# Query, key and attention weights turned by VectorE blocks and a DRAM round trip instead of TensorE, in a hybrid attention layer on one core

## The chip, the core and the metric

The kernel runs on one core of a Trainium2 chip. Five engines matter: TensorE (PE in the profile, with its weight loads as PEld), VectorE (DVE), ScalarE (ACT), GpSimd (POOL, which here only issues DMAs that add to their target) and SyncE (SP, which issues most DMAs). The metric is the device time of one execution in microseconds. A median over three runs is given.

## What is computed

One layer for 512 tokens of width 2048, in float32. The input is normalized and multiplied by one wide matrix. Its columns give, for three branches with four heads of 128 columns each, a query, a key, a value and a gate (4 x 128 columns a head), and for each branch 2048 merge gates.

```
A: p = softmax(q k^T / sqrt(128) + forget bias, causal);  o = p v     (q, k normalized)
B: p = softmax(q k^T / sqrt(128) + bias by distance);     o = p v     (q, k normalized)
C: p = stick-breaking weights of q k^T / sqrt(128);       o = p v
y      = o * silu(gate)                  for every head
merged = sum over branches of sigmoid(merge gate) * (y_branch @ w_up)
out    = x + merged @ w_out
```

The forget bias of A is a running sum over the log of a per-token gate that is computed from the input as well (the "forget sums").

## The kernel before, in words

**Matmuls.** Every float32 operand is split into an upper and a lower part of reduced precision, and a product is three matmuls (upper by upper, lower by upper, upper by lower), so a tile of 128x128 by 512 costs three. All large ones are issued by `mm` (line 266). The work is cut into *units*: each takes a weight chunk of 256x512 (512 KB), splits it on ACT into the upper part (`wh`, line 376) and on DVE into the lower part (`wl`, line 386), and multiplies. Two units are prepared ahead of the one that runs (`LA`, three buffers of `wh`, two of `wl`), and eight raw chunks (`raw`, `NR`) are loaded ahead on SP's queue (line 278).

**Input projection.** The 24 column groups of 512 (12 heads, 12 gate groups) are taken in this order: the first head plain (`first_head`, 9 units), the first gate group plain (8 units), and then eleven pairs of one gate group and one head (`head`). A pair is done by Strassen's scheme with seven products of four units each (`Strassen`, 28 units). The products come in the order 5, 1, 6, 7, 4, 2, 3 (`PLAIN`, line 592). Their sums are made in `after` (line 644): product 5 is copied from PSUM by ACT and kept for product 7; 7 and 4 finish the head's halves, 2 and 3 the gate group's. For four of the products the weight chunks are sums: those of 5 and 7 are summed by a second, adding DMA on POOL's queue (line 282), those of 6 and 3 by DVE (line 588). Finished gate groups are scaled and stored to DRAM (`spill`, line 1161), to be read again for the merge.

**Attention.** A head arrives as four tiles `c` of 128 tokens x (query, key, value, gate). For A and B, query and key are normalized (`norms`). `qk` turns query and key so that the head dimension lies on the partitions: four PE transposes into a PSUM bank each (`turned`, line 873), then ACT and DVE make the upper and lower part from PSUM. `values` splits the values block by block (lines 907 and 909). `gate` turns the gate in another way: DVE turns 32x32 blocks (line 920), SP stores them to DRAM (line 923), and four DMAs on ACT's queue (line 930) read them back so that the blocks land in their turned places; each piece read is one row of 32 numbers. The last head turns its gate on PE. `soft_scores` or `stick_scores` make the weights `p`, one block of 128 queries at a time, against 128 to 512 keys. `soft_trans` turns them on PE (line 1019; 4 + 3 + 2 + 1 turns a head) and splits them, and `av` multiplies with the values (lines 1107 to 1109). The last head adds its causal mask by a small matmul on PE (line 988), the other A heads on DVE (line 991).

**Order of the work.** The order of the instructions on PE, ACT and DVE is written out when the kernel is built, by a planner (`Flow`). Each piece of work is a generator that yields the engine and the time that it is taken to need, buffers, or events; the planner always takes the piece that can start first, by its own clock, and each engine then runs its queue in that order. A DMA has a planned landing time (`landing`, line 271):

```
        line[0] = max(line[0], ready) + 0.5
        line[1] = max(line[1], line[0] + 1.0) + kb / 370.0
        return line[1] + 1.5
```

If data land later than planned, the engine that has the reading instruction next in its queue stands, and everything behind it. SP and ACT issue DMAs in order too. Attention is hung onto the units by `at`: `stages` (line 1124) gives each step a distance in units from the point where the head is finished, by the offsets `OFF` (line 1523) for scores, turned weights and values.

**PSUM** has eight banks: four for products (`acc`), four for side work (`att`).

**After the projection** come 24 units for the up-projection with the merge gates, whose merged result is turned on PE too (line 1357, 64 turns), and two Strassen tasks of 28 units for the output.

Of the kernel before, what the change touches and what calls it, by code (L numbers as in the profile page):

```python
# [36 lines left out]
Q, K, V, G = 0, 1, 2, 3  # L37
# [126 lines left out]
def hybrid_kernel(  # L164
# [22 lines left out]
    pa = ctx.enter_context(tc.tile_pool(name="pa", bufs=4, space=PS))  # L187
    pt = ctx.enter_context(tc.tile_pool(name="pt", bufs=4, space=PS))
# [9 lines left out]
    t2s, atts, raws, xps = Slots(NT, KEPT), Slots(4), Slots(NR), Slots(NX)  # L198
    accs, wls = Slots(4), Slots(LA)
# [16 lines left out]
    def blk(i):  # L216
        return slice(i * P, (i + 1) * P)
# [62 lines left out]

    def add_up(to, src, ready, kb):
# [26 lines left out]
    onef, zerof, nu_f = tmpc[:, blk(0)], tmpc[:, blk(1)], tmpc[:, blk(2)]  # L308
# [5 lines left out]
    identb = cp.tile([P, P], BF16, name="identb")  # L314
    nc.vector.tensor_copy(identb, identf)

    mska = cp.tile([P, P], BF16, name="mska")
    nc.gpsimd.affine_select(out=nu_f, in_=zerof, pattern=[[-1, P]], base=0, channel_multiplier=1,
                            compare_op=ALU.is_ge, fill=NEG)
    nc.vector.tensor_copy(mska, nu_f)  # L320

# [270 lines left out]
    PLAIN = [(p, c) for p in (5, 1, 6, 7, 4, 2, 3) for c in range(CH)]  # L592

    class Strassen:
# [9 lines left out]
        def __init__(self, src, ops, done, order=PLAIN, other=(), rest=None):  # L604
            self.src, self.ops, self.done, self.rest = src, ops, done, rest
            self.order, self.other = order, other
            self.ps, self.ev = {}, {}
# [36 lines left out]
        def after(self, p, tb, slots):  # L644
# [8 lines left out]
            if p in (1, 5):  # L653
                yield t2s, 1
                c = t2("v" if p == 5 else "u")
                yield ACT, act_us(S)
                nc.scalar.activation(c, ps, AF.Copy)
                (v if p == 5 else u)[tb] = c
                give(slots)
                set_(self.event(p, tb))  # L660
# [9 lines left out]
            elif p == 7:  # L670
                yield self.event(6, tb)
                yield t2s, 1
                u3[tb] = t2("w")
                yield d
                add(u3[tb], u2[tb], ps)
                give(slots)
                yield self.event(5, tb)
                yield d
                add(u2[tb], u2[tb], v[tb])
                spawn(self.left("c12", tb, lambda r: add(u2[tb], u2[tb], r)), 4.0, flow.fin)  # L680
                yield d
                minus(v[tb], u3[tb], v[tb])
                spawn(self.left("c21", tb, lambda r: sub(u3[tb], r, u3[tb])), 4.0, flow.fin)
                spawn(self.left("c22", tb, lambda r: add(v[tb], v[tb], r)), 4.0, flow.fin)
                yield self.event("c22", tb)
                finished("c22", v[tb])
# [130 lines left out]
    class Head:  # L817
        def __init__(self, n, h, last=False):
            self.n, self.h, self.last = n, h, last
# [3 lines left out]
            self.c, self.t, self.ev, self.count = [None] * QB, {}, {}, {}  # L823

# [19 lines left out]
        def taken(self):  # L844

            if self.nth("taken", 4):
                give(t2s, QB)

# [19 lines left out]
        def turned(self, r):  # L868

            yield PE, 0.11 * QB  # L870
            ps = att()
            for tb in range(QB):
                nc.tensor.transpose(ps[:, blk(tb)], self.c[tb][:, blk(r)], identf)  # L873
            self.taken()
            return ps

        def qk(self, r):
            if self.n == C:
                yield from self.all_there()
            else:  # L880
                yield self.event("n", r)
            yield t2s, 2
            self.t[r] = pair_of("qk")
            yield atts, 1
            ps = yield from self.turned(r)
            h, lo = self.t[r]
            if self.n == C:
                yield from split(h, lo, ps, S)
            else:
# [3 lines left out]
                nc.scalar.activation(h, ps, AF.Copy, scale=g)  # L893
                yield DVE, dve_us(S)
                nc.vector.scalar_tensor_tensor(lo, ps, g, f(h), op0=ALU.mult, op1=ALU.subtract)
            give(atts)
            set_(self.event("p", r))

        def values(self):
            yield from self.all_there()  # L900
# [3 lines left out]
            for tb in range(QB):  # L904
                c = self.c[tb][:, blk(V)]
                yield ACT, act_us(P)
                nc.scalar.activation(h[:, blk(tb)], c, AF.Copy)
                yield DVE, dve_us(P)
                nc.vector.tensor_sub(lo[:, blk(tb)], c, f(h[:, blk(tb)]))
            self.taken()  # L910
            set_(self.event("v"))

        def gate(self):
            yield from self.all_there()
            yield t2s, 1
            if not self.last:
                t = t2("gt")
                for tb in range(QB):
                    yield DVE, 0.3
                    nc.vector.transpose(t[:, blk(tb)], self.c[tb][:, blk(G)])  # L920
                self.taken()
                gd = dp.tile([4 * QB, 32, P], F32, name=nm("gd"))
                nc.sync.dma_start(gd.rearrange("(t a) r c -> (a r) t c", a=4), t.rearrange("p (t c) -> p t c", t=QB))
                stored(t2s, 1, 256)
# [649 lines left out]
```

## Time and profile before

| what | value |
|---|---|
| runs | 1301.43 us median of 3 (1301.05 to 1301.47) |
| profiled execution: span of its instructions | 1300.1 us |
| instructions | 17368 |
| PE busy | 1294.1 us |
| DVE busy | 1069.5 us |
| ACT busy | 748.2 us |
| DMA moved | 284.39 MB, mean 219 GB/s |

The profile gives the profiled execution by its span; the median of the runs is 1.3 us above it. The profile's page counts each engine's busy time; issuing DMAs is not counted. A row of a group reads: line, engine, operation, output<-input, shapes, count | busy us, mean ns of one | idle time before it and who ended it. A row of the chain reads: start us, length us, what. A row of waits reads: who waited for whom: us in total, times, longest. A row of a window reads: from:to, its length, then busy us (and instructions) of PE, PEld, DVE, ACT and POOL, then PE's granted clock, the DMA engines' mean share and GB/s. A row of the DMA queues reads: packets, MB, share of the span of sixteen engines; a row of DMA issues ends with the KB of one and its median time from issue to landing.

### The profile page before, as it was taken

To read this page: it belongs to the slowest core of one execution; us is meant where nothing else is said; L and a number is where in the kernel's file an instruction comes from. 1 tells how busy PE (TensorE), PEld (TensorE's weight loads), DVE (VectorE), ACT (ScalarE), POOL (GpSimd) and SP (SyncE) were. 2 spreads that over 40 slices of the span, in tenths; PEclk is the share of its full clock that TensorE was granted. 3 is DMA by queue.
4 is the path that set the end of the run, shared out by engine and by line. 5 is a ranking of instruction groups with operands and counts; after the bars stand their busy time and mean duration, and the time that the engine had idled before them with its cause. 6 is when DMAs were issued, how large, how long until landed. Compare 5 with 4: busy or idle time off the path is not lost.

```text
span 1300.1 us, 17368 instructions
## 1 busy us (share of the span) xinstructions
PE 1294.1 (100%) x5941; PEld 1075.1 (83%) x5941; DVE 1069.5 (82%) x1607; ACT 748.2 (58%) x1259; POOL 92.0 (7%) x116
## 2 busy tenths in 40 slices
PE   9999999999999999999999999999999999999998
PEld 8888888888888888888888888888888888888887
DVE  7966797898989888898886886978879668698767
ACT  7745465565557646576466664666658546463442
POOL 0001000110011001110011000110000000000110
PEclk9999999999999999999999999999999999999999
DMA  9855687896788989888787777877796756738983
GB/s 358 256 147 145 185 230 194 230 239 215 218 238 237 250 236 272 236 240 240 205 249 175 222 213 191 252 162 208 224 282 194 264 194 196 177 93 258 250 245 126
DMA packets 124072, 284.39 MB, mean 219 GB/s; under 512 B 34368, under 2 KB 40144, under 8 KB 123984
## 3 DMA queue, kind: packets, MB, share of 16 engines
q1 hardware_dynamic: 83328, 221.42, 50.7%
q0 software_dynamic: 14976, 54.53, 23.1%
q10 hardware_dynamic: 25680, 7.34, 2.3%
q8 instruction: 46, 0.75, 0.2%
q14 instruction: 42, 0.34, 0.1%
HBM read 260.66 MB, written 22.59 MB: 218 GB/s over the span
## 4 chain that ended last, share of the span: by engine, by line
PE 99%; DMA 1%; DVE 0%; issue 0%; ACT 0%; ACTq 0%
PE acc L266 93%; PE att L1019 1%; PE att L873 1%; DMA gl<-u 1%; PE att L1109 1%; PE att L1108 1%; PE att L261 1%; PE att L262 1%; PE att L263 1%; PE att L1357 1%; PE att L1107 1%; PE att L430 0%; DVE s L702 0%; DVE u L1161 0%; DVE gt L920 0%
## 5 line engine op out<-in xcount | busy, mean ns | idle before, releaser
L376 ACT ACTIVATE wh<-raw 128x1024 fp32r<-128x1024 f32 (+1 forms) x404 | 426.9, 1057 | 412.6 <-PE acc L266 317.6
L386 DVE TENSOR_TENSOR wl<-raw,wh 128x1024 fp32r<-128x1024 f32 (+1 forms) x405 | 492.6, 1218 | 159.1 <-PE acc L266 110.6
L266 PE MATMUL acc<-wh,x 128*128 128x512 f32 x1664 | 428.7, 392 | 0.1
L266 PEld LDWEIGHTS acc<-wh,x 128*128 128x128 f32 x1664 | 310.2, 188 | 62.8 <-issue 0.3
L266 PE MATMUL acc<-wh,t 128*128 128x512 f32 x1056 | 272.4, 391 | 0.0
L266 PE MATMUL acc<-wl,x 128*128 128x512 f32 x832 | 230.7, 391 | 0.0
L266 PEld LDWEIGHTS acc<-wh,t 128*128 128x128 f32 x1056 | 197.1, 188 | 40.3
L266 PEld LDWEIGHTS acc<-wl,x 128*128 128x128 f32 x832 | 155.4, 188 | 32.3 <-DVE wl L386 0.2
L266 PE MATMUL acc<-wl,t 128*128 128x512 f32 x528 | 148.0, 392 | 0.0
L282 POOL DMA_DIRECT2D raw<-in_w_col x88 | 76.1, 865 | 867.6 <-ACT wh L376 209.0
L588 DVE TENSOR_TENSOR raw<-raw,raw 128x1024 f32<-128x1024 f32 x104 | 126.4, 1218 | 0.1
L266 PEld LDWEIGHTS acc<-wl,t 128*128 128x128 f32 x528 | 98.3, 188 | 19.7
L266 PE MATMUL acc<-wh,m 128*128 128x512 f32 x448 | 112.9, 389 | 0.0
L266 PE MATMUL acc<-wh,y 128*128 128x512 f32 x384 | 103.1, 390 | 0.0
L266 PEld LDWEIGHTS acc<-wh,m 128*128 128x128 f32 x448 | 84.1, 188 | 17.4
L266 PEld LDWEIGHTS acc<-wh,y 128*128 128x128 f32 x384 | 72.0, 188 | 15.0
L266 PE MATMUL acc<-wl,m 128*128 128x512 f32 x224 | 62.5, 390 | 0.0
L266 PE MATMUL acc<-wl,y 128*128 128x512 f32 x192 | 59.5, 391 | 0.0
L266 PEld LDWEIGHTS acc<-wl,m 128*128 128x128 f32 x224 | 41.9, 188 | 8.8 <-DVE wl L386 0.2
L266 PEld LDWEIGHTS acc<-wl,y 128*128 128x128 f32 x192 | 35.8, 188 | 7.1
L247 ACT ACTIVATE ah<-att 128x512 fp32r<-128x512 f32 (+3 forms) x48 | 20.9, 436 | 31.7 <-PE att L1019 31.6
L1323 DVE TENSOR_TENSOR sg<-acc,sg 128x512 f32<-128x512 f32 x48 | 32.9, 690 | 5.0 <-PE acc L266 2.6
(182 smaller groups left out, 1119.9 us busy)
## 6 DMA issues: line engine op xcount, KB each, us to landing
raw<-in_w_col SPq DMA_DIRECT2D x235, 512.0 KB, 5.0
raw<-in_w_col POOLq DMA_DIRECT2D x88, 512.0 KB, 8.2
raw<-in_w_out SPq DMA_DIRECT2D x40, 512.0 KB, 4.1
raw<-in_w_up SPq DMA_DIRECT2D x24, 512.0 KB, 3.8
sg<-gl SPq DMA_DIRECT2D x48, 256.0 KB, 4.8
xf<-in_xn SPq DMA_DIRECT2D x32, 256.0 KB, 6.7
raw<-in_w_out POOLq DMA_DIRECT2D x16, 512.0 KB, 6.5
gl<-u SPq DMA_DIRECT2D x22, 256.0 KB, 9.9
```

The source lines that it names most:

```text
L247: nc.scalar.activation(hi, src, AF.Copy)
L261: nc.tensor.matmul(ps, lh, rh, start=start, stop=False, skip_group_check=more)
L262: nc.tensor.matmul(ps, lh, rl, start=False, stop=False, skip_group_check=more)
L263: nc.tensor.matmul(ps, ll, rh, start=False, stop=stop, skip_group_check=more)
L266: nc.tensor.matmul(ps, w, x, start=start, stop=stop, skip_group_check=more)
L282: nc.gpsimd.dma_start(to, src, accum_op=ALU.add)
L376: nc.scalar.activation(u.hi, u.raw, AF.Copy)
L386: nc.vector.tensor_sub(u.lo, u.raw, f(u.hi))
L588: nc.vector.tensor_add(to.raw, to.raw, self.raw)
L873: nc.tensor.transpose(ps[:, blk(tb)], self.c[tb][:, blk(r)], identf)
L1019: nc.tensor.transpose(ps[:, blk(i)], self.p[i][:, blk(j)], identf)
L1323: nc.vector.tensor_mul(t, ps[tb], t)
```

## The change

- The columns of a head are laid out as query, key, gate, value. `crossed` turns the 32x32 blocks of query, key and gate in place on DVE, 384 columns at once, and stores the whole tile to DRAM (SP). `back` reads query, key or gate so that the blocks land turned, by four DMAs on ACT's queue; `qk_in` splits query and key from there, `gate_in` takes the gate. `values` reads the values from the stored tile (SP) and splits them in one piece.
- The weights `p` are turned in blocks in place by DVE and stored (`sent`), and read back turned by four DMAs each on SP (`soft_in`).
- Side work has two PSUM banks instead of four, products have six; product 5 stays in PSUM until it is used.
- Two heads run plain first. Ten pairs of gate group and head follow, with the products in the order 5, 1, 6, 2, 3, 7, 4, so that the gate group is finished first; the last pair is two gate groups in the old order. The offsets in `stages` are larger and the same for all heads.
- The last head is treated like the others: no mask matmul, its `y` goes through DRAM.

```diff
-Q, K, V, G = 0, 1, 2, 3
+Q, K, G, V = 0, 1, 2, 3
...
-    pa = ctx.enter_context(tc.tile_pool(name="pa", bufs=4, space=PS))
-    pt = ctx.enter_context(tc.tile_pool(name="pt", bufs=4, space=PS))
+    pa = ctx.enter_context(tc.tile_pool(name="pa", bufs=6, space=PS))
+    pt = ctx.enter_context(tc.tile_pool(name="pt", bufs=2, space=PS))
...
-    t2s, atts, raws, xps = Slots(NT, KEPT), Slots(4), Slots(NR), Slots(NX)
-    accs, wls = Slots(4), Slots(LA)
+    t2s, atts, raws, xps = Slots(NT, KEPT), Slots(2), Slots(NR), Slots(NX)
+    accs, wls = Slots(6), Slots(LA)
 
...
-    PLAIN = [(p, c) for p in (5, 1, 6, 7, 4, 2, 3) for c in range(CH)]
+    PLAIN = [(p, c) for p in (5, 1, 6, 2, 3, 7, 4) for c in range(CH)]
+    LAST = [(p, c) for p in (5, 1, 6, 7, 4, 2, 3) for c in range(CH)]
...
+            if p == 5:
+                v[tb] = ps
+                set_(self.event(5, tb))
...
+                if self.gates_first:
+                    yield self.event(3, tb)
+                    u3[tb] = u2[tb]
...
+                yield t2s, 1
+                c = t2("v")
+                yield d
+                minus(c, u3[tb], v[tb])
+                give(slots)
...
+            elif p == 3 and self.gates_first:
+                yield self.event(6, tb)
+                yield t2s, 1
+                w = t2("w")
+                yield d
+                add(w, u2[tb], ps)
+                give(slots)
+                set_(self.event(3, tb))
                 yield self.event(5, tb)
                 yield d
+                add(w, w, v[tb])
+                set_(self.event("w", tb))
+                spawn(self.left("c12", tb, lambda r: add(w, w, r)), 4.0, flow.fin)
+                yield self.event("c12", tb)
+                finished("c12", w)
...
-        def turned(self, r):
-
-            yield PE, 0.11 * QB
-            ps = att()
-            for tb in range(QB):
-                nc.tensor.transpose(ps[:, blk(tb)], self.c[tb][:, blk(r)], identf)
...
+        def crossed(self):
...
+            self.pd = dp.tile([QB, P, S], F32, name=nm("pd"))
+            d = self.d = dp.tile([QB, P, S], F32, name=nm("qd"))
+            for tb in range(QB):
+                yield DVE, dve_us(3 * P) + 0.07
+                c = self.c[tb]
+                nc.vector.transpose(c[:, :3 * P], c[:, :3 * P])
+                nc.sync.dma_start(d[tb], c)
+                sent = landing(flow.fin, 256)
+                t2s.free.append(sent)
+            self.event("x").t = sent + LATER
+
+        def back(self, r, t):
+            for b in range(4):
+                yield ACT, 0.48
+                src = self.d.rearrange("t (a r) c -> (t a) r c", r=32)[:, :, r * P + 32 * b:r * P + 32 * (b + 1)]
+                nc.scalar.dma_start(t[32 * b:32 * (b + 1), :].rearrange("p (n c) -> p n c", c=32),
+                                    src.rearrange("n r c -> r n c"))
+            return Event(landing(flow.fin, 512) + 1.0)
+
+        def qk_in(self, r):
...
             yield t2s, 2
-            self.t[r] = pair_of("qk")
-            yield atts, 1
-            ps = yield from self.turned(r)
-            h, lo = self.t[r]
+            self.t[r] = h, lo = pair_of("qk")
+            t = f(lo)
+            ev = yield from self.back(r, t)
+            yield ev
...
+        def gate_in(self):
+            yield self.event("x")
...
         def values(self):
-            yield from self.all_there()
+            yield self.event("x")
...
-            for tb in range(QB):
-                c = self.c[tb][:, blk(V)]
...
-                nc.vector.tensor_sub(lo[:, blk(tb)], c, f(h[:, blk(tb)]))
...
-        def gate(self):
...
-                    yield DVE, 0.3
-                    nc.vector.transpose(t[:, blk(tb)], self.c[tb][:, blk(G)])
...
+            yield fetch_as(f(lo), self.d[:, :, V * P:].rearrange("t p c -> p t c"), 256)
+            yield from split(h, lo, f(lo), S, self.event("v"))
...
-            yield from self.turn()
+            if self.prev is not None:
+                yield self.prev.event("d", QB - 1)
...
-            if self.last:
-                nc.tensor.matmul(ps[:, blk(i)], identb, mska, start=False, stop=True)
-            elif n == A:
+            if n == A:
...
-        def soft_trans(self, j):
+        def sent(self, i):
+
+            yield self.event("s", i)
+            m = (i + 1) * P
+            yield DVE, dve_us(m) + 0.07
+            p = self.p[i]
+            nc.vector.transpose(p, p)
+            nc.sync.dma_start(self.pd[i, :, :m], p)
+            self.gone[i] = landing(flow.fin, m / 2)
+            set_(self.event("d", i))
...
+        def soft_in(self, j):
+            for i in range(j, QB):
+                yield self.event("d", i)
+            yield Event(max(self.gone) + LATER)
             yield from self.parts_of(j)
-            yield atts, 1
-            yield PE, 0.11 * (QB - j)
-            ps = att()
-            for i in range(j, QB):
...
+            h, lo = self.hl[j]
+            n = S - j * P
+            for b in range(4):
+                src = self.pd[j:].rearrange("t (a r) c -> (t a) r c", r=32)[:, :, j * P + 32 * b:j * P + 32 * (b + 1)]
+                nc.sync.dma_start(f(lo)[32 * b:32 * (b + 1), :].rearrange("p (n c) -> p n c", c=32),
+                                    src.rearrange("n r c -> r n c"))
+            yield Event(landing(flow.fin, n) + 1.0)
+            yield from split(h, lo, f(lo), n, self.event("a", j))
...
         def stages(self):
 
             one = lambda fn, i: lambda: fn(i)
...
+            soft = self.n != C
+            s, t, o = (OFF[k + ("" if soft else "c")] for k in "sto")
+            scores, start = (self.soft_scores, self.soft_start) if soft else (self.stick_scores, self.stick_start)
+            g = [(0, self.norms)] if soft else []
+            g += [(1, self.crossed), (s - 4, one(self.qk_in, K)), (s - 3, one(self.qk_in, Q)), (t - 2, self.gate_in)]
+            g += [(s - 2 if soft else s - 1, start)]
+            g += [(s + i, one(scores, i)) for i in range(QB)]
+            g += [(t - 3, self.values), (t, self.silu)]
+            g += [(s + i, one(self.sent, i)) for i in range(QB)]
+            g += [(t + i, one(self.soft_in, i)) for i in range(QB)]
             g += [(o + i, one(self.av, i)) for i in range(QB)]
             return g
...
-    def first_head():
-        hd = Head(C, 0)
...
+    def first_heads():
+        for h in range(2):
+            hd = Head(C, h)
...
+            parts = [[k, k + 1] for k in range(0, KT, 2)]
+            units.extend(quad([[0], [1]] + parts[1:] if h == 0 else parts, group(C, h), done, h == 0))
+            u0 = len(units)
+            for d, g in hd.stages():
+                at(u0 + 1 + (2 * d // 3 if h == 0 else d), g)
...
-        units.extend(quad([[k, k + 1] for k in range(0, KT, 2)], gate_group(0), gates_done))
...
-    def head(n, h, i, last=False):
...
-        groups = gate_group(i), group(n, h)
+        two_gates = hd is None
+        groups = gate_group(GATES[i]), gate_group(GATES[i + 1]) if two_gates else group(hd.n, hd.h)
...
-        units.extend(Strassen(src, ops, done).units)
-        at(u0 + 5 * CH - 1, lambda: brow(i))
-        for d, g in hd.stages():
-            at(u0 + 5 * CH + d, g, (4.0 if g in (hd.gate, hd.values, hd.silu) else 0.3) if last else 5.0)
...
+        units.extend(Strassen(src, ops, done, LAST if two_gates else PLAIN).units)
+        at(u0 + 3 * CH - 1, lambda: brow(GATES[i]))
+        if two_gates:
+            at(u0 + 3 * CH, lambda: brow(GATES[i + 1]))
+        else:
+            for d, g in hd.stages():
+                at(u0 + 6 * CH + d, g, HSLACK)
+
+    GATES = [n * NQ + g for n in (C, B) for g in range(NQ)] + [A * NQ + g for g in (0, 2, 1, 3)]
+    first_heads()
+    for i, (n, h) in enumerate([(C, 2), (C, 3)] + [(n, h) for n in (B, A) for h in range(NH)]):
+        last_head = Head(n, h)
+        pair_task(i, last_head)
+    pair_task(NB * NQ - 2)
...
-OFF = dict(cs=4, ct=12, co=14, s=8, t=14, o=16, s1=3, t1=4, o1=5)
+OFF = dict(sc=12, tc=20, oc=22, s=12, t=20, o=22)
+LATER = 2.5
+HSLACK = 8.0
```

More of the change, by code (lines that the diff above doesn't have):

```diff
@@ L606, in __init__ @@
             self.order, self.other = order, other
+            ps = [p for p, _ in order]
+            self.gates_first = ps.index(3) < ps.index(7)
             self.ps, self.ev = {}, {}
@@ L1030, in stick_start @@
         def stick_start(self):
-            yield from self.turn()
+            if self.prev is not None:
+                yield self.prev.event("d", QB - 1)
             yield t2s, 3
```

186 lines of the change are left out of this document (62 added, 124 removed).

## The prediction

> **What bounds the kernel now.** I read the page's first part first, to see which engine has no room. The runs shown have a median of 1301.43 us; the profiled execution has a span of 1300.1 us, so 1.3 us lie around the span, and I carry them unchanged.
>
> ```profile
> span 1300.1 us, 17368 instructions
> ...
> PE 1294.1 (100%) x5941; PEld 1075.1 (83%) x5941; DVE 1069.5 (82%) x1607; ACT 748.2 (58%) x1259; POOL 92.0 (7%) x116
> ```
>
> TensorE (PE) is busy for all but 6.0 us. The waits of PE alone come next, then the chain that ended last, in order of time:
>
> ```profile
> PE att L430 <- DVE mskf L302: 1.1, 1, 1.1
> PE att L261 <- ACT p L1049: 0.9, 1, 0.9
> ```
>
> ```profile
> 871.52 40.41 PE acc L266 x178
> 911.93 0.44 PE att L873 x4
> ...
> 914.68 0.44 PE att L873 x4
> ...
> 937.06 0.44 PE att L1019 x4
> ...
> 940.27 0.33 PE att L1019 x3
> ...
> 953.80 29.99 PE acc L266 x132
> ```
>
> PE waits twice in the whole run, 2.0 us together; the other 4 us are the start and the end. The chain is PE work back to back. One head's task, from the piece at 871.52 to the same piece at 953.80, takes 82.28 us; its large matmuls go at 40.41/178 = 0.227 us each. So anything taken from PE's queue shortens the run by as much, as long as nothing else becomes late.
>
> **The change part by part.** *Removed from PE.* The turns of query, key and the last gate (line 873) and of the attention weights (line 1019), and the last head's mask matmuls (line 988):
>
> ```profile
> L1019 PE MATMUL att<-identf,p 128*128 128x128 f32 x120 | 20.9, 272 | 0.0
> L873 PE MATMUL att<-identf,v 128*128 128x128 f32 x46 | 8.8, 273 | 0.0
> L873 PE MATMUL att<-identf,w 128*128 128x128 f32 x46 | 8.8, 272 | 0.0
> L873 PE MATMUL att<-identf,c 128*128 128x128 f32 x8 | 1.2, 272 | 0.0
> L988 PE MATMUL att<-mska,identb 128*128 128x128 bf16 x4 | 0.9, 230 | 0.0
> ```
>
> ```profile
> 998.96 0.23 PE L988 MATMUL att<-mska,identb 128*128 128x128 bf16 x1
> 999.00 0.36 PE L261 MATMUL att<-qkh,qkh 128*128 128x256 f32 x1
> ```
>
> The 272 ns are start to end; neighbours overlap. What a turn takes of the queue is in the chain above: 0.44/4 and 0.33/3, so 0.11 us. With 120 + 46 + 46 + 8 = 220 turns that is 24.0 us (0.109 each; 24.2 at 0.11). A mask matmul holds the next one up by 0.04 us, four of them 0.2 us. The term is 24.2 us.
>
> *Moved on PE.* Two heads run plain first, instead of a head and a gate group; of the other groups ten pairs are gate with head and one is gate with gate. Before: two plain groups and eleven pairs. After: the same. So the large matmuls stay, and the order of products within a pair (5, 1, 6, 2, 3, 7, 4) costs PE nothing by itself. The score and value matmuls stay too. PE's sum is 1294.1 - 24.2 = 1269.9 us, the span 1275.9, the time 1277.2.
>
> *Added to VectorE.* Per head four turns of 128x384 (query, key, gate) and one each of 128, 256, 384 and 512 columns (weights), all in 32x32 blocks; one lower part of the values of 512 columns in place of four of 128; the gate's own four turns go. The block turn shows at one width only; for the others I take the elementwise rows and the ratio at 128 columns, 304/283 = 1.07.
>
> ```profile
> L920 DVE STREAM_TRANSPOSE gt<-w 128x128 f32<-128x128 f32 x20 | 6.1, 304 | 0.0
> ...
> L909 DVE TENSOR_TENSOR vl<-v,vh 128x128 fp32r<-128x128 f32 x22 | 6.2, 284 | 0.0
> ...
> L991 DVE TENSOR_TENSOR att<-att,mskf 128x128 f32<-128x128 f32 x12 | 3.2, 288 | 0.0
> ...
> L1067 DVE TENSOR_TENSOR p<-p,lk 128x512 f32<-128x512 f32 x4 | 2.7, 683 | 0.0
> ...
> L1067 DVE TENSOR_TENSOR p<-p,lk 128x384 f32<-128x384 f32 x4 | 2.2, 550 | 0.0
> ...
> L1067 DVE TENSOR_TENSOR p<-p,lk 128x256 f32<-128x256 f32 x4 | 1.7, 418 | 0.0
> ...
> L1067 DVE TENSOR_TENSOR p<-p,lk 128x128 f32<-128x128 f32 x4 | 1.1, 283 | 0.0
> ```
>
> Turns: 4 x 0.59 + 0.30 + 0.45 + 0.59 + 0.73 = 4.4 us. Values: 0.68 - 4 x 0.28 = -0.45. Gate: -4 x 0.304 = -1.2. Together +2.8 us a head, with the last head's masks about +35 us in all: DVE goes from 1069.5 to 1105 us, 87% of the shorter span. PE covers it; none is on the path.
>
> *ScalarE (ACT).* It loses the copy of product 5, which now stays in PSUM, and gains twelve DMA issues a head where it had four (the last head none): 100 more.
>
> ```profile
> L657 ACT ACTIVATE v<-acc 128x512 f32<-128x512 f32 x26 | 14.9, 586 | 4.8 <-PE acc L266 4.8
> ```
>
> ```profile
> L930 ACTq DMA_DIRECT2D g<-gd x44: 309/500/608, 75.9 to 925.8; - x44
> ```
>
> Less 14.9 us of work, 100 x 0.5 = 50 us more of issuing, on an engine that is busy for 58%. Nothing on the path.
>
> *PSUM.* Banks for side work go from four to two, for products from four to six. Where the merged rows are turned, PE now runs sixteen turns in one go:
>
> ```profile
> 1041.13 1.75 PE att L1357 x16
> ```
>
> With two banks the third and fourth group wait for an ACT copy (like the 0.586 us above) unless products stand between. Bound: 0, or 2 x 0.6 us at each of four such places, 4.8 us. It might even gain, as six product banks end waits; but PE shows 2 us of waits in all, so a gain is at most 2 us. I take 0: the planner orders PE's queue with the bank count known to it, and it has matmuls to put between.
>
> *The DRAM trips.* Per head four stores of 256 KB, four of 64 to 256 KB, reads of 128-byte pieces for query, key, gate and weights, and a 256 KB read of the values. The gate's trip before is the only such trip in the trace.
>
> ```profile
> q1 hardware_dynamic: 83328, 221.42, 50.7%
> ...
> q10 hardware_dynamic: 25680, 7.34, 2.3%
> ```
>
> ```profile
> gl<-u SPq DMA_DIRECT2D x22, 256.0 KB, 9.9
> gl<-s SPq DMA_DIRECT2D x22, 256.0 KB, 5.9
> ...
> gd<-gt SPq DMA_DIRECT2D x11, 256.0 KB, 11.6
> g<-gd ACTq DMA_DIRECT2D x44, 64.0 KB, 2.9
> ```
>
> Queue q1 pays 0.507 x 16 x 1300.1 us for 221.42 MB, 47.6 us of one engine per MB, 3.0 us of all sixteen. On q10 the 44 reads make 44 x 512 = 22528 pieces of 128 bytes (2.88 MB); the other 4.46 MB at q1's price take 212 of its 478 us, which leaves 11.8 ns a piece. After: 12 x (3 x 2048 + 10 x 512) = 135168 pieces, 112640 more, 83 us of all sixteen. Whole rows: 12.6 + 7.9 + 3.1 - 2.9 + 0.5 MB, about 21 MB, 63 us. Together 146 us of DMA time, 12.2 us a head.
>
> *Waits added.* Four reads on ACT's queue wait for the stores; what stands behind them is the copies into the upper weight parts (line 376), for which PE waits. The weights' reads stand on SP's queue, ahead of the coming weight loads. The planner charges a store 0.5 + 1.0 + 256/370 + 1.5 = 3.7 us when the line is free (lines 271 to 275), and the change adds 2.5 before the first read: 6.2 us.
>
> ```profile
> ACT wh L376 <- PE acc L266: 317.6, 203, 5.7
> ```
>
> ```profile
> 0.00:30.00 30.00, 28.77 (x142) 24.12 (x143) 20.59 (x38) 22.56 (x46) 2.08 (x12) 1.00 0.96 355
> ...
> 360.00:460.00 100.00, 100.00 (x467) 83.17 (x465) 89.58 (x147) 61.05 (x107) 10.36 (x12) 1.00 0.88 242
> ```
>
> ```profile
> 500.00:511.00 11.00, 11.00 (x54) 9.14 (x53) 10.19 (x16) 6.04 (x10) 0.86 (x1) 1.00 1.06 311
> ```
>
> ```profile
> 841.00:852.00 11.00, 11.00 (x54) 9.29 (x53) 9.94 (x26) 8.41 (x18) 0.00 (x0) 1.00 0.45 124
> ```
>
> ```profile
> 60.00:1000.00 940.00, 939.05 (x4318) 780.39 (x4316) 789.94 (x1196) 556.88 (x957) 74.20 (x86) 1.00 0.79 219
> ```
>
> In these window rows the last three numbers are PE's granted clock, the DMA share and GB/s. The clock stays at 1.00. ACT stands ahead of PE by 317.6/203 = 1.6 us on average at a weight copy and by up to 5.7; that covers a late landing. A store lands late when the DMA share is high (1.06 at 500 to 511, where weights of the next pair load) and early when it is 0.45. With heads finished by the last two products, the stores fall into the next pair's first product, the 0.45 stretch. So I take 6 us for a store, near gl<-s, which the planner's 6.2 holds. For what gets through I put 2.8 us: one wait of 0.9 us, like the one in the trace, for every fourth read of weights or keys that PE needs, three such waits. Forecast: 1277.2 + 2.8 = 1280.0 us, its own range 1276 to 1284 (below: no new wait and 1 us of PE's old ones gone; above: the 4.8 us of PSUM and part of the 2.8).
>
> *A rule that speaks against it.* The trace has a turn of four blocks on PE at 0.44 us and a trip of 11.6 + 2.9 = 14.5 us for the same block by DVE and DRAM. The Trainium skill, "VectorE: DVE Perf Modes", sections "The three transpose paths" and "Rules for kernel authors", says that VectorE turns 32x32 blocks only, that a 128x128 turn belongs on TensorE where PSUM will do as its target, and warns of strided DMA copies as turns. By that rule the change goes the wrong way; the trace agrees on the latencies, 14.5 against 0.44 us, but has PE as the one engine without room. What it would do here is the third rival.
>
> **The rivals.** *DMA becomes the bound (0.17).* From 60 to 1000 us the share is 0.79; with 146 us more in 917 us it is (743 + 146)/917 = 0.97. In the stretch with the forget sums, 0.88 x 82.28 + 12.2 = 84.6 us in a task of 80.3 us, over 1.05. For it: that is no room. Against: packets overlap and the share reached 1.06 with PE fully busy. If the ceiling is the 0.96 of the first 30 us, a task there takes 84.6/0.96 = 88.1 us, 7.8 more than 80.3; the eight forget sums stand 15 units apart, 120 units or some four tasks of 28, so 31 us: 1308 at the worst, about 1293 if the eight weight buffers carry half of it.
>
> *VectorE late (0.07).* In the row for 360 to 460 it has 89.6 of 100 us; with 3.4 more and 2.4 us less of time it has 95%. It works in order, so bunched turns delay the lower weight parts. Some 3 us in four tasks make 12 us: 1289 to 1292. Against: it was at 10.19 of 11 beside a full PE at 500 to 511.
>
> *Late landings, slower than before (0.15).* If a store takes 11.6 us, as gd<-gt did, the first read stands 11.6 - 6.2 = 5.4 us in ACT's queue; the weight copies behind it have 1.6 us of cover, so PE stops for 3.8 us in each of twelve heads, 46 us: 1323 us. It decides from 24.2/12 = 2.0 us of stop per head, a landing of 9.8 us; gl<-u with 9.9 is just there. Against: those were measured in the saturated stretch.
>
> That the change does not take the turns off PE is excluded by its text: no turn is left on lines 873 and 1019.
>
> **How the numbers follow.** Forecast 0.61; DMA 0.17, of which 0.02 ends near the old time and 0.03 above; VectorE 0.07; late landings 0.15, of which 0.02 ends near it. A difference of 0.2% (2.6 us) is about what a measurement of this kernel can tell from none. Faster 0.61 + 0.12 + 0.07 = 0.80, same 0.02 + 0.02 = 0.04, slower 0.03 + 0.13 = 0.16. The range leaves out the slower cases, half of the near ones and 0.02 below: 1276 to 1299.
>
> **What would show it.** Right: about 5717 matmuls on PE, PE near 1270 us, PE's waits below 6 us, a task of about 80.3 us between like pieces of the chain, DVE near 1105 us, DMA share in the middle near 0.95, some 135,000 pieces of 128 bytes. Wrong: PE waiting on wh or on the lower parts of query, key or weights (landings), on weight loads by the raw tiles (DMA), or a task longer than 82.28 us.

## The result and the profile after

The changed kernel takes 1423.46 us (median of four runs, 1419.07 to 1425.20), the kernel before 1301.45 us beside it (four runs as well). The ratio is 1.0934, with a 95% interval from 1.0916 to 1.0951: the change makes the kernel 9.3% slower. The profiled execution took 1419.07 us. Its page begins so, and the fourth row of its slices below is the clock that PE was granted:

```profile
span 1417.4 us, 17651 instructions
...
PE 1302.1 (92%) x5717; PEld 1064.8 (75%) x5717; DVE 1093.8 (77%) x1625; ACT 729.0 (51%) x1196; POOL 91.6 (6%) x115
...
PEclk9999799899998999999999999798999899999999
...
q1 hardware_dynamic: 162480, 250.54, 53.4%
q0 software_dynamic: 14976, 54.53, 20.2%
q10 hardware_dynamic: 78480, 13.90, 5.5%
```

The work left PE as it should: 5717 matmuls where there were 5941. But PE now stands for 1417.4 - 1302.1 = 115.3 us, where it stood for 6.0, and its busy time is 1302.1 us where the sum of steps had 1269.9. Those two differences, 109.3 and 32.2 us, are the whole distance from the predicted span of 1275.9 us without waits to 1417.4. PE's waits name what comes late:

```profile
PE acc L266 <- ACT wh L372: 78.0, 16, 16.7
PE att L1128 <- ACT ah L247: 12.0, 3, 5.0
PE acc L266 <- DVE wl L382: 10.3, 7, 6.8
```

78.0 of the 115.3 us are waits for `wh`, the copy that ACT makes of weights just loaded. ACT itself is busy for half of the span, so the next view is what ACT waits for ahead of that line:

```profile
ACT wh L372 <- PE acc L266: 238.1, 153, 4.4
ACT wh L372 <- DMA qkl<-qd: 68.8, 9, 22.4
ACT wh L372 <- DMA raw<-in_w_col: 65.0, 28, 8.7
...
ACT ah L247 <- DMA al<-pd: 36.2, 27, 6.4
```

The wait for `qkl<-qd` is not one for data of the copy: the nine waits of up to 22.4 us are the issues of the reads of query and key (line 913), which stand in ACT's queue ahead of the copy. The chain that ended last, around the longest stop, shows why such an issue stands:

```profile
864.47 22.46 PE acc L266 x99
887.11 0.58 SPq L1040
887.74 0.69 SPq L1040
888.48 7.88 SPq L1040
...
899.82 2.20 DMA al<-pd
902.04 0.31 ACTq L913
902.47 1.07 ACT wh L372
903.58 10.47 PE acc L266 x35
```

Read from below: PE resumes at 903.58 when a copy on ACT ends; that copy stood behind a read's issue; the issue waited for reads of the attention weights (`al<-pd`, line 1040), which SP had issued for the head before, one of them taking 7.88 us to issue. The two reads share neither data nor queue. What they share is in the trace's records of the instructions: the DMAs of SP and ACT together signal their landing on eight semaphores (numbers 101, 102 and 104 to 109; POOL's DMAs have eight others), given out in turn in the order in which the program writes the DMAs. A DMA waits until the one before it on the same semaphore has landed, even where that one is in the other queue and has not been issued yet. All stands of ACT before line 913 make some 100 us in these records, and some 65 of them end with a read of attention weights. The three longest:

```
ACT stands, us      waits on semaphore   held by a read of attention weights that SP issued at
138.39 to 157.50    101                  148.74
880.09 to 900.11    105                  887.11
955.51 to 973.11    104                  967.63
```

So SP had issued those three reads only 10.4, 7.0 and 12.1 us into the stands. Each time it had just waited for a store of attention weights, which had taken 9.1, 6.5 and 9.8 us to land. Over the whole run SP stood in this way for 55.5 us:

```profile
SPq L1040 <- DMA pd<-p: 55.5, 14, 12.7
```

The stands on ACT are thus made of three things: an order that binds ACT's queue to SP's, late stores, and late reads.

The windows around the second one show what it costs (PE busy, PEld, DVE, ACT, POOL, then the granted clock, the DMA share and GB/s):

```profile
880.00:885.00 5.00, 5.00 (x24) 4.14 (x23) 2.92 (x4) 0.09 (x1) 1.24 (x2) 1.00 1.04 413
885.00:890.00 5.00, 1.92 (x9) 1.26 (x7) 0.00 (x0) 0.00 (x0) 1.36 (x2) 1.00 1.06 308
890.00:895.00 5.00, 0.00 (x0) 0.00 (x0) 0.00 (x0) 0.00 (x0) 0.86 (x1) 0.60 1.11 220
895.00:900.00 5.00, 0.00 (x0) 0.00 (x0) 0.00 (x0) 0.00 (x0) 0.00 (x0) 0.50 0.94 165
900.00:905.00 5.00, 1.42 (x3) 1.16 (x4) 0.92 (x2) 2.52 (x3) 0.00 (x0) 0.50 0.76 117
905.00:910.00 5.00, 5.00 (x16) 3.59 (x15) 4.97 (x6) 3.61 (x6) 0.00 (x0) 0.70 0.56 119
```

The DMA engines are full (1.04 to 1.11) with weight loads and POOL's adds when the reads are issued. PE then stands for 16.7 us, and ACT and VectorE with it, and when PE starts again its clock is at half (0.50 in the row from 900 to 905, 0.70 in the next): 16 matmuls from 905 to 910, where there were 24 from 880 to 885.

The landings after, as the medians from issue to landing:

```profile
qkl<-qd ACTq DMA_DIRECT2D x96, 64.0 KB, 4.4
...
qd<-v SPq DMA_DIRECT2D x20, 256.0 KB, 5.4
vl<-qd SPq DMA_DIRECT2D x12, 256.0 KB, 6.4
g<-qd ACTq DMA_DIRECT2D x48, 64.0 KB, 12.8
pd<-p SPq DMA_DIRECT2D x12, 256.0 KB, 6.5
al<-pd SPq DMA_DIRECT2D x48, 64.0 KB, 3.4
pd<-p SPq DMA_DIRECT2D x12, 192.0 KB, 8.1
```

By their medians the stores of heads and weights land in 3.7 to 8.1 us, near the 6 us of the prediction, but single stores of weights take up to 15.3 us. A gate's read takes 12.8 us, where such a read took 2.9 us before.

### The profile page after: what moved, and what is told of

It reads as the page before. It is cut to its first block, busy times and chain, and to the rows that moved or that the text cites. A ratio compares the mean times of both kernels' runs of the same rounds, so it can differ in the third digit from the quotient of the medians.

```text
span 1417.4 us, 17651 instructions
## 1 busy us (share of the span) xinstructions
PE 1302.1 (92%) x5717; PEld 1064.8 (75%) x5717; DVE 1093.8 (77%) x1625; ACT 729.0 (51%) x1196; POOL 91.6 (6%) x115
## 3 DMA queue, kind: packets, MB, share of 16 engines
q1 hardware_dynamic: 162480, 250.54, 53.4%
q0 software_dynamic: 14976, 54.53, 20.2%
## 5 line engine op out<-in xcount | busy, mean ns | idle before, releaser
L266 PE MATMUL acc<-wh,x 128*128 128x512 f32 x1664 | 433.2, 397 | 60.9 <-ACT wh L372 60.9
L266 PEld LDWEIGHTS acc<-wh,x 128*128 128x128 f32 x1664 | 316.0, 191 | 132.2 <-ACT wh L372 67.5
L266 PEld LDWEIGHTS acc<-wh,t 128*128 128x128 f32 x1056 | 200.0, 190 | 59.5 <-ACT wh L372 18.0
L266 PE MATMUL acc<-wl,x 128*128 128x512 f32 x832 | 235.4, 395 | 1.0 <-DVE wl L382 0.7
L266 PE MATMUL acc<-wl,t 128*128 128x512 f32 x528 | 151.0, 395 | 8.5 <-DVE wl L382 8.4
L247 ACT ACTIVATE ah<-al 128x512 fp32r<-128x512 f32 (+3 forms) x48 | 21.6, 464 | 36.2 <-DMA al<-pd 36.2
L251 DVE TENSOR_TENSOR al<-al,ah 128x512 fp32r<-128x512 f32 (+3 forms) x48 | 22.5, 487 | 23.0 <-ACT ah L247 22.8
```

Source lines behind the costliest of these rows:

```text
L247: nc.scalar.activation(hi, src, AF.Copy)
L251: nc.vector.tensor_sub(lo, src, f(hi))
L266: nc.tensor.matmul(ps, w, x, start=start, stop=stop, skip_group_check=more)
```

## The experiments

Each kernel here was run once, beside a run of the kernel before on the same chip (1301.2 to 1301.6 us every time). The changed kernel's own four runs spread over 6 us, so smaller differences between kernels with trips are not read. Four theories were held against each other: **T1**, the shared landing semaphores; **T2**, the small pieces themselves land late among weight loads and adds; **T2'**, the planner counts on the trips too early, so engines that work in order stand; **T3**, the new order and the two side banks cost by themselves.

### The parts by themselves: order, query and key, weights

The order alone: query, key and weights turned on PE as before, with two side banks, the new order, and the trip of gate and values kept. In this kernel, and wherever query and key are back on PE, the tile is stored only after they have been turned, so the trip that is left starts later than in the change.

```
-  crossed: nc.vector.transpose(c[:, :3 * P], ...)      qk_in: reads of qd      sent / soft_in: pd
+  crossed: nc.vector.transpose(c[:, blk(G)], ...)      qk_in: nc.tensor.transpose(ps[:, blk(tb)], self.c[tb][:, blk(r)], identf)
+  soft_trans: nc.tensor.transpose(ps[:, blk(i)], self.p[i][:, blk(j)], identf)
```

> Query, key and attention weights are turned on TensorE as before (two side banks of PSUM); what stays of the change is the order of heads and gate groups, the order of products, the PSUM split and the trip of the tile for gate and values. Theory T1 (the eight landing semaphores that SP's and ACT's DMAs share let too few DMAs be in flight, so that a read on ACT's queue waits for an unrelated one of SP): with 288 fewer reads and 48 fewer stores the stalls go; the 24 us of turns are back, so 1300 to 1310 us. T2 (the 128-byte pieces land late because the DMA engines are full): few pieces are left, also 1300 to 1310. T3 (the new order and the two PSUM banks stall TensorE by themselves): stays above 1380 us.

Measured: 1351.87 us, which no theory had: the order costs 50 us with all the turns on PE, and the trips, with the turns off PE, 72 more. By the planner's own clock this kernel's PE ends 1.7 us after that of the kernel before (1293.3 against 1291.6), so nearly all of the 50 us is work that comes later than planned. ACT waits for the gate's read:

```profile
ACT y L1095 <- DMA g<-qd: 34.5, 7, 7.6
```

The two trips were then tried one at a time. First only the weights back on PE:

> Only the attention weights go back to TensorE; query, key, gate and values still make the DRAM trip. T1: the three longest stands of ACT all waited for a read of weights; with 192 reads and 48 stores gone they go, TensorE idles below 15 us, 1290 to 1305 us. T2: 61 thousand of 135 thousand pieces go, so about half of the loss: near 1350 us. T3: above 1380 us.

Measured: 1352.06 us, as with both back. This is T2's figure and well above T1's, but T2 had the run with both back 40 us faster, so the share of the pieces alone does not explain it. Then only query and key back on PE:

> Only query and key go back to TensorE; gate, values and attention weights make the DRAM trip. T1: ACT issues 48 reads instead of 144, SP's 192 reads of weights stay; the stands of ACT before gate reads stay, those before query and key reads go: 1320 to 1370 us. T2: 49 thousand of 135 thousand pieces go, a third of the loss: near 1375 us. T3: above 1380 us.

Measured: 1418.67 us, 0.4 us under the fastest of the changed kernel's runs, and above the figures of T1 and T2 (T3 had it above 1380, but not the two runs ahead of it). So, on this order, the trip of query and key moves nothing on balance (the 96 turns that it takes off PE bring nothing), and the trip of the attention weights carries all of the 67 to 72 us. In that last kernel no stand on ACT is longer than 12 us; the same loss comes there as many small ones:

```profile
ACT ah L247 <- DMA al<-pd: 67.3, 35, 4.8
ACT wh L372 <- DMA raw<-in_w_col: 60.7, 27, 6.6
ACT y L1106 <- DMA g<-qd: 39.2, 7, 9.2
```

### The shared semaphores

The reads of query, key and gate on POOL's queue, whose DMAs have semaphores of their own:

```
-                yield ACT, 0.48
-                nc.scalar.dma_start(t[32 * b:32 * (b + 1), :]...
+                nc.gpsimd.dma_start(t[32 * b:32 * (b + 1), :]...
```

> The change as it is, but the reads of query, key and gate are issued on POOL's queue, which has landing semaphores of its own, instead of ACT's. T1: ACT cannot stand before issuing a read; the stands of 19.1, 20.0 and 17.6 us go, with them 46 us of TensorE's idle time and some of the low clock: 1340 to 1365 us or below. T2: the same pieces land as late, and ACT stands before the copy that uses them: 1400 to 1430 us.

Measured: 1428.05 us, so T1 as the one cause falls: the three long stands were gone and the loss was not. But this edit had also taken the reads' cost out of the planner, which wrote another order whose own clock ended at 1302.0 instead of 1279.9. So the move was made again with the issue alone changed and every instruction in its old order:

> The change, with the reads of queries, keys and gates issued on POOL's queue instead of ACT's, and every other instruction in the order of the changed kernel (the earlier move of these reads also let the planner write another order, whose own clock ended 22 us later). T1, the landing semaphores that SP's and ACT's DMAs share: ACT has no DMA left, so its three stands of 17.6 to 20.0 us go, with the clock that they cost: 1350 to 1380. T2, the landings of small pieces themselves: the same data is late on another queue, 1400 to 1430.

Measured: 1387.03 us, 36 less than the change, 7 us above T1's range and 13 below T2's. The move also takes 144 issues of some 0.4 us each off ACT's queue, so the 36 us are not the semaphores' alone. ACT's waits in it show both what went and what stayed:

```profile
ACT wh L372 <- PE acc L266: 259.8, 163, 4.4
ACT wh L372 <- DMA raw<-in_w_col: 119.2, 48, 9.3
ACT ah L247 <- DMA al<-pd: 73.6, 39, 10.3
```

Ahead of the copies no wait for `qkl<-qd` is left, and no stand of ACT reaches 12 us; the waits for attention weights have grown from 36.2 to 73.6 us and those for weight loads from 65.0 to 119.2. With the stall gone, ACT reaches the next late thing. Last, the reads of attention weights were put on POOL's queue as well:

> The change, with the reads of queries, keys, gates and attention weights all on POOL's queue, order as in the changed kernel. T1: SP has only stores and plain loads left, so a weight load no longer waits behind a read of attention weights; 1320 to 1360. T2: 1395 to 1430. A third way: POOL's queue is served in order, so the adds of weights wait behind a read that waits for its store; then adds land late and PE waits for the split of sums, over 1420.

Measured: 1432.36 us, the time of the third way, but its mechanism is not shown. The reads on POOL do wait for their stores (most of such idle time of POOL costs nothing by itself):

```profile
POOL al L1040 <- DMA pd<-p: 131.1, 7, 53.3
```

But weight loads are not what comes late: ACT waits 96.7 us for them, less than the 119.2 of the run above. PE waits for the copy of the attention weights, 12.0 us in the change:

```profile
PE att L1128 <- ACT ah L247: 56.8, 15, 10.9
```

The reads of the weights land there at medians of 3.5 to 6.8 us by their size, on SP's queue in the change at 1.9 to 3.4.

### The small pieces

Whole rows of 2 KB or less are read in place of 128-byte pieces, as many reads on the same queues. The turned layout is not made: queries, keys, gates and attention weights hold other values. A read also takes its rows from one stored tile in place of up to four.

```
-                nc.scalar.dma_start(t[32 * b:32 * (b + 1), :].rearrange("p (n c) -> p n c", c=32), src.rearrange("n r c -> r n c"))
+                nc.scalar.dma_start(t[32 * b:32 * (b + 1), :], self.d[b, :32, :])
-                nc.sync.dma_start(f(lo)[32 * b:32 * (b + 1), :].rearrange("p (n c) -> p n c", c=32), src.rearrange("n r c -> r n c"))
+                nc.sync.dma_start(f(lo)[32 * b:32 * (b + 1), :], self.pd[QB - 1, 32 * b:32 * (b + 1), :n])
```

> The whole change with the planner's times as they are and as many DMAs, but each read of query, key, gate and weights takes contiguous rows of 512 to 2048 bytes instead of pieces of 128 bytes: the turned layout is not made, so the attention's numbers mean nothing. If the small pieces are what makes reads late (T2): below 1340 us. If the number of DMAs and the landing semaphores are (T1): above 1390 us. T2': between, by as much as reads land sooner.

Measured: 1381.39 us, 42 less, between the two. The reads land sooner, the gate's at a median of 6.0 us (12.8 in the change), those of query and key at 3.0 (4.4). The long stands stay, at the same three places (18.6, 16.1 and 17.0 us), each until a read of attention weights has landed, and PE still waits for `wh`:

```profile
PE acc L266 <- ACT wh L372: 51.2, 11, 15.7
```

```profile
ACT wh L372 <- DMA qkl<-qd: 60.9, 8, 21.8
```

So the size of the pieces does not make those stands; the order on the shared semaphores is unchanged here, and with the reads on POOL the stands were gone. Both cures in one:

> The change with whole rows read in place of 128-byte pieces (the turned layout is not made, so queries, keys, gates and attention weights hold other values) and the reads of queries, keys and gates on POOL's queue. Both causes taken away together: T1 and T2 together expect 1310 to 1345. If the order and the two side banks hold most of the loss (T3), it stays near the 1352 of the order alone or above.

Measured: 1356.92 us, 66 less than the change, 12 above the range of T1 with T2, and by 5 above the order alone, where T3 had it. Together the two causes hold 66 of the 72 us. The trips still do not pay: this kernel has 216 turns fewer on PE than the order alone, some 24 us by the prediction's own price, and is not faster.

### The planner's times

Later times for the planner: 8 us in place of 2.5 behind a store, and 8 in place of 1 behind a read's landing.

```
-LATER = 2.5                                  -  landing(flow.fin, 512) + 1.0
+LATER = 8.0                                  +  landing(flow.fin, 512) + 8.0      (the same in soft_in)
```

On the whole change:

> The whole change, but the planner is told that the data come later: 8 us instead of 2.5 after the stores, 8 us instead of 1 on top of its landing time for the reads of query, key, gate and weights. T2' (the loss is the planner's: it puts the instruction that reads the data into ACT's, DVE's or TensorE's queue for a time at which the data are not there, and the weight copies behind it stand): most stalls go, TensorE idles below 30 us instead of 115, 1290 to 1330 us. T1 (shared landing semaphores): ACT's reads still stand before they are issued, 1370 to 1430 us.

Measured: 1472.33 us, worse than any theory had it. The reads' issues on ACT now stood for 11 to 21 us in six heads, each on a semaphore held by a read of attention weights that SP issued only 10 to 14 us into the stand; a part of the loss is planned (the planner's own clock ends at 1303.6 instead of 1279.9). On the order alone, where only the gate's trip is left to be late:

> The kernel with the new order and every turn of query, key and weights on TensorE, with the planner's times for the gate's trip 8 us later (store 8 instead of 2.5, read 8 on top instead of 1). T2': the five stands of ACT of 5 to 9 us before the silu are gone; TensorE idles below 15 instead of 40 us; 1300 to 1318 us. T3 (the new order and the two side banks cost by themselves): stays near 1350 us.

Measured: 1330.52 us, 21 less than with the early times, between T2' and T3. ACT's waits for the gate (34.5 us with the early times, at a median landing of 8.6 us) are gone, so I put 21 of the order's 50 us down to its late read; the planner wrote another order with the later times, and that part is not separated. And with the weights back on PE:

> Attention weights on TensorE; query, key, gate and values by DRAM, with the same later times. T2': 1288 to 1310 us, below the kernel before if all stalls go (11 us of turns are saved). T1 or T3: 1335 to 1355 us.

Measured: 1364.50 us, 12 worse than with the early times and above both ranges. Whether later times only fail because of the shared semaphores was the next question: later times with the reads on POOL's queue, and the same with whole rows.

> The change with the reads of queries, keys and gates on POOL's queue, and the planner told later times (8 us in place of 2.5 and of 1.0 for a store and a read to land; its own clock then ends at 1303.6 with 43 us of PE idle planned). T2', the times were too early: the stands before weights of attention (74 us of ACT for 39 waits with the queue moved alone) go, 1315 to 1345. If the transfers are too late for any order: the planned 23 us come on top, 1385 to 1415.

> As the run beside it, with whole rows read in place of 128-byte pieces (the turned layout is not made, so queries, keys, gates and attention weights hold other values). T2': everything arrives by the planned time, 1310 to 1325, some 10 us over the planner's own end as in the kernel before. If the times are not the cause: 1350 to 1380.

Measured: 1436.05 and 1397.66 us, above both theories' ranges, so T2' falls for the trips. In the first of them the waits for attention weights did shrink, from 73.6 to 43.7 us, as told; but other loads came late in their place. PE's waits there:

```profile
PE acc L266 <- ACT wh L372: 23.7, 12, 5.2
PE acc L266 <- DVE sg L1339: 21.8, 1, 21.8
PE att L1130 <- DVE al L251: 17.5, 2, 11.0
```

The loss moves to other loads.

### The two side banks

The kernel before with six accumulators and two side banks, and nothing else:

```
-    pa = ... bufs=4      pt = ... bufs=4      atts = Slots(4)      accs = Slots(4)
+    pa = ... bufs=6      pt = ... bufs=2      atts = Slots(2)      accs = Slots(6)
```

> The kernel before, with two side banks and six accumulators in place of four and four, and nothing else. If two side banks cost PE by themselves (T3): 1312 to 1332, which would be most of the 29 us that the order with later gate times leaves. If not: 1300 to 1305 (the planner's own clock ends 1.3 us later).

Measured: 1307.13 us, 6 us more, between the two ranges. PE waits at the scores for a side bank that the forget sums (`fl`) hold:

```profile
PE att L261 <- DVE fl L749: 4.6, 2, 2.4
```

## Why the prediction was wrong

It said 1280.0 us, between 1276 and 1299, and faster with 0.80. By its own steps:

- *Removed from PE, 24.2 us.* Right in kind: 5717 matmuls, as forecast. The busy time came out at 1302.1 us, not 1270. Weighted with the granted clock, in windows of 2 us, it is 1280.2 us: 22 of the 32 us are matmuls at a lowered clock; the cause of the other 10 stays open. "The clock stays at 1.00" was read from a trace in which PE never stood, and the sum had no term for what a stop does to it.
- *Added to VectorE.* Right: 1093.8 us (forecast 1105). The block turns took what the elementwise rows said, or a little less: 0.56 us for 384 columns (0.59 forecast), 0.70 for 512 (0.73):

```profile
L902 DVE STREAM_TRANSPOSE v<-v 128x384 f32<-128x384 f32 x20 | 11.1, 560 | 0.0
...
L1024 DVE STREAM_TRANSPOSE p<-p 128x512 f32<-128x512 f32 x12 | 8.4, 700 | 0.6 <-ACT p L1015 0.5
```

- *The DRAM trips, 146 us of all sixteen engines.* Right in size: q1, q0 and q10 held 50.7, 23.1 and 2.3% of 1300.1 us before (989 us) and hold 53.4, 20.2 and 5.5% of 1417.4 us (1121 us), 132 more. As an average it never became the bound, and the time is far above the first rival's 1308. What counted was the stretch: full engines just where the trip has to come back. A part of that rival's sign is there all the same: ACT's waits for weight loads rose from 41.0 to 65.0 us.
- *PSUM at 0, bound 4.8 us.* The two banks cost 6 us by themselves: I took the wrong end, and the wrong place (PE waits at the scores, beside the forget sums, not where the merged rows are turned).
- *The order "costs PE nothing by itself".* This step failed: the order, with the gate's and values' trips, costs 50 us with every turn on PE. If the parts add up, the banks are 6 of it and the gate's late read 21. Some 23 us are left open; in the run with later times for the gate PE stands 20 us more than before, half of it for the lower weight parts (`wl`), the first row of its waits:

```profile
PE acc L266 <- DVE wl L382: 9.9, 8, 4.7
```

  Taken by itself this already outweighs the 24.2 us that the turns bring. A smaller part was in the plan: for the whole change the planner's own clock for PE ends 11.7 us earlier than for the kernel before (1279.9 against 1291.6), with 19.5 us of PE idle where it had 6.6. The sum carried over the 6 us of idle time.
- *Waits added, 2.8 us.* The step that failed most: "I take 6 us for a store, near gl<-s, which the planner's 6.2 holds". The medians kept near it, single stores did not (up to 15.3 us, and SP stood 55.5 us for them). What I priced at nothing was everything behind the store: the reads' own landings in a full stretch (small pieces, worth 42 us by themselves), and the wait of an issue for an unrelated DMA (36 us by itself, with the issues moved; the two overlap and hold 66 together). In place of 2.8 us, PE stood 109.3 us more than before. Of the first, the rows of before gave a median of 2.9 us and single reads of up to 8.3. The second they did not show: ACT's longest stand before line 930 was 1.3 us, for a store of its own data.
- *The third rival, late landings, 0.15.* Right in its sign and its place (a read stands in ACT's queue, the weight copies behind it come late, PE stops) and wrong in what is late and in size: 46 us were forecast for stops of 3.8 us in twelve heads, against 78.0 us in 16 waits of up to 16.7 for the copies alone. It decided by the landing of the store at 9.8 us. The medians stayed under that, single stores did not, and the reads behind them were not in it at all. The rule of the Trainium skill quoted there, which has such turns on TensorE ("VectorE: DVE Perf Modes", "Rules for kernel authors"), held for this kernel as far as it was tried.

What is shown: that both the reads' issue on ACT behind shared semaphores and the small pieces cost, that on this order the weights' trip and not query's and key's carries the loss, and that the order has a price of its own. What stays open: how much of the 36 us is the semaphores' and how much the issues' on ACT, what makes the same loss where query and key are on PE and the long stands are missing, 23 us of the order, 10 us of PE's busy time, and why later times for the planner move the loss to other loads, beyond the PE idle time that its plan already holds. The trips on the old order were not tried. The best version with the new order, all turns on PE and later times for the gate, is 29 us slower than the kernel before, so by these runs the turns are better left on PE.

## What to carry to other kernels

A DMA had three waits here: for its data, for what stands in its queue, and for whatever else uses its landing semaphore, issued or not. Before adding many small DMAs, count how many are in flight, with whom they share it, and in which order the program writes them. Price a trip through memory by its landing, store and read, in the stretch where it must come back, with the DMA share of that stretch, not by a median over the run. When PE has no idle time, price each new stop at its length plus the slow clock behind it, and test a rewritten order with the old work in it before crediting the work that it makes room for.

## What the runs showed of the hardware

*A DMA issue is held by a DMA of another queue.* Eight landing semaphores for the queues of SP and ACT together let at most eight of their DMAs be under way. An issue on ACT stood for up to 20.0 us until an unrelated read of SP had been issued (after 7.0 of them) and had landed. Single issues of SP's reads of weights (line 1040) took up to 7.88 us in place of 0.45, the median of the 192.

*The clock after a stop.* A stop of 4.7 us, from 643.30 to 648.01, is followed by 3.4 us at half clock:

```profile
648.00:649.00 1.00, 0.99 (x3) 0.56 (x4) 0.68 (x1) 1.00 (x2) 0.00 (x0) 0.81 0.48 75
649.00:650.00 1.00, 1.00 (x3) 0.81 (x4) 0.34 (x1) 0.63 (x2) 0.00 (x0) 0.50 0.49 76
650.00:651.00 1.00, 1.00 (x4) 0.81 (x4) 0.22 (x1) 0.17 (x1) 0.00 (x0) 0.50 0.32 50
...
652.00:653.00 1.00, 1.00 (x7) 0.91 (x6) 0.00 (x0) 0.14 (x1) 0.00 (x0) 0.98 0.44 111
```

Here the clock falls just after PE has begun again (in the long stop above it fell while PE stood), and the half lasts from 648.62 to 652.04. The Trainium skill, "TensorE: Matmul & The Clock Gate", section "Why this matters for your kernels", says to leave no gap of PE above some 3 us. The eight stops of 4.7 us and more in this trace agree: the half clock came in or right after each. Shorter ones give no sharp limit: one of 3.3 us (at 339.56) and one of 2.3 (at 569.33) were not followed by it, another of 2.3 (at 733.67) and one of 2.1 (at 353.10) were.
